# A decoder layer on one core: x, c and the bias vectors laid out by features before the launch, the first norm from squares and ones products, the opening in another order

## Chip, core and metric

The kernel runs on one core of a Trainium2 chip. The metric is the device time of one execution in microseconds (us), the median of several runs. Engines: TensorE (PE in the profile, its weight loads PEld), VectorE (DVE), ScalarE (ACT), GpSimd (POOL) and SyncE (SP), which only issues DMAs here.

## What is computed

One layer of a decoder for 1024 prompt tokens and 8 sample tokens, D = 1024 features, hidden width 2816, all in float32. What matters here is the first of its three norms and the first up-projection:

```python
mod = (silu(c) @ ada_w + ada_b).reshape(B, 9, D)      # c: one row for the prompt, one for each sample
def pre(i, t):                                         # i = 0, 1, 2
    return rms_norm(t, norm_g[i]) * (1 + mod[3*i+1]) + mod[3*i]
x = x + 0.5 * mod[2] * swiglu(pre(0, x), ffn1_up, ffn1_down)
y, states = token_mix(pre(1, x), ...)                  # attention and gated branch
x = x + mod[5] * y
x = x + 0.5 * mod[8] * swiglu(pre(2, x), ffn2_up, ffn2_down)
y_prompt, y_sample = rms_norm(x, final_g)
```

## The kernel before

**Layout and pieces.** Activations lie by features: partition = feature within a block of 128, eight blocks k. Tokens lie in two halves p of 516 columns, each two quarters q of 258 (256 prompt tokens and 2 samples); the sample columns are the `ends` of a quarter. `XT[p][h]` holds features 4h to 4h+3 of half p. Matmuls run in three parts: an operand is split into a high part and a low remainder (`high` on ScalarE, `low` on VectorE), and hi*hi, hi*lo, lo*hi are added up, so a block of four k is 12 matmuls of 128 x 258 (L743 to L745).

**First up-projection.** `Up.run` goes through 22 column blocks n. Blocks 0 and 1 go plainly, half by half, in turns (0, p=0), (1, p=0), (0, p=1), (1, p=1) of eight steps each; steps 0 to 3 need features 0 to 3 (h = 0) of the half, steps 4 to 7 features 4 to 7, and after each of the last four the PSUM result is read (L767, L768, L771). From block 2 on a turn has seven products over both halves (of 24 matmuls), whose operands `blend` makes from sums and differences of the blocks of x (eight passes of VectorE over 1032 columns for each half). `prepare` splits weights ahead of their use.

**What sets the order.** The program order on each engine is written out. Within a block, `tick` is called after each second k, so twice in a step; each tick advances the generators of `hi_q` by one `yield`. `require` advances them at once where a step needs what they make.

**The opening (L1012 to L1176).** SyncE loads ada weights of groups 0 and 2, four row tiles of x, the first up weights, ada groups 1 and 3, the second up weights, the other four row tiles. c, the ada bias and the norm weights come as rows and are transposed on TensorE (`silu_c`, L447). Each ada group gives four blocks of features of the modulation: `first_mods` (8 matmuls), a copy, four transposes, three steps on VectorE (`ada_fin`, L416). Groups 0 and 2 are shift and scale of features 0 to 3 of the first norm, groups 1 and 3 of features 4 to 7. For each row tile t, `row_scale` sums squares along the row on ScalarE and VectorE, `over_rms` scales the row, `turned_x` transposes it, `modulate` reads PSUM, scales and shifts. The samples go the same way (`sample_rows`, `sample_norm`). Steps 0 to 3 of the first turn are written in between, step 0 and 1 ahead of ada group 3. The second half of the tokens follows as `second_half` in `hi_q`; in it `raw_x` (L1028) also transposes all eight unscaled row tiles, copies them out of PSUM and stores them to `xs_d`, from where `Down` (L843) loads the residual; only then come `blend(0)` and `blend(1)`.

**The other norms.** `pair_norm` (L625) makes norms 2 and 3 from x by features: `rstd` (L499) sums squares over partitions by products with a column of ones, takes the power on GpSimd, and small products spread the result over partitions (L630); then for each block a VectorE pass (L642) and a ScalarE pass (L643), and after four blocks one copy of the sample columns (L645).

Of the kernel before, what the change touches and what calls it, by code (L numbers as in the profile page):

```python
# [15 lines left out]
D = 1024  # L16
# [18 lines left out]
def const_block():  # L35
    c = np.zeros((128, C_END), np.float32)
    i = np.arange(128)
    neg = np.float32(-1e30)
    c[:, C_ID:C_ID + 128] = np.eye(128)
    c[:, C_MP:C_MP + 128] = np.where(i[None, :] >= i[:, None], 0, neg)  # L40
    c[:, C_MO:C_MO + 128] = np.where(i[None, :] <= i[:, None], 0, neg)
    c[:, C_M0:C_M0 + 128] = c[:, C_MO:C_MO + 128]
    same = (i[None, :] // 64) == (i[:, None] // 64)
    c[:, C_M2:C_M2 + 128] = np.where(same & (i[None, :] <= i[:, None]), 0, neg)
    for j in range(2):
        for h in range(2):
            c[2 * j + h, C_SEL + j * 128 + h * 64:C_SEL + j * 128 + h * 64 + 64] = 1
    for hh in range(4):
        c[:, C_SX + hh] = (i % 32) == hh
        c[:, C_BM + hh] = (i // 32) == hh  # L50
    return c
# [14 lines left out]
def trunk(ctx: ExitStack, tc, a, o):  # L66
# [72 lines left out]
    START = dict(sc=(4, 6, 5, 5), pt=(7,), ms=(6,), tr=(6, 7), nx=(0, 1, 2, 3))  # L139
# [209 lines left out]
    ada0, xin, XT = {}, {}, {}  # L349
# [34 lines left out]
    XS = cpool.tile([P, 8, 8], FT, name="XS")  # L384
# [62 lines left out]
    def silu_c():  # L447
        q = ps_ms()
        nc.tensor.transpose(q[:, :104], rows[:104, :128], ident[:104, :104])
        nc.vector.tensor_copy(RT, q[:, :104])  # L450
        q = ps_pt()
        for k in range(8):
            nc.tensor.transpose(q[:, k * 16:k * 16 + 9], crow[:, k * 128:(k + 1) * 128], ident[:9, :9])
        nc.vector.memset(ph[:, 256:512], 0.0)
        qv = q[:, :128].rearrange("p (k t) -> p k t", k=8)[:, :, :9]
        th = tt()
        t3 = th[:, :72].rearrange("p (k t) -> p k t", k=8)
        nc.scalar.activation(t3, qv, AF.Tanh, scale=0.5)
        nc.vector.scalar_tensor_tensor(t3, t3, 1.0, qv, op0=ALU.add, op1=ALU.mult)
        nc.vector.tensor_scalar(scf[:, :, :9], t3, 0.5, None, op0=ALU.mult)  # L460

    def row_stat(row, w, ss, n):

        for h in range(2):
            e = tt()
            v = row[:, h * 512:(h + 1) * 512]
            if h:
                nc.vector.scalar_tensor_tensor(e[:w, :512], v, 1.0, v, op0=ALU.mult, op1=ALU.mult,
                                               accum_out=ss[:w, 4 + n:5 + n])
            else:  # L470
                nc.scalar.activation(e[:w, :512], v, AF.Square, accum_out=ss[:w, n:n + 1])

    def row_rstd(ss, w, i, n):
        r = R0[:w, i:i + n]
        nc.vector.tensor_tensor(r, ss[:w, :n], ss[:w, 4:4 + n], op=ALU.add)
        nc.vector.tensor_scalar(r, r, 1.0 / D, EPS, op0=ALU.mult, op1=ALU.add)
        nc.gpsimd.tensor_tensor(r, r, nhalf[:w, :n], op=ALU.pow)
# [147 lines left out]
    def pair_norm(i, p, b0, blocks, slow):  # L625

        x = XT[p]
        rs = yield from rstd(p, BLOCKS, 4 if blocks and p else 5, 2 if p else 3)
        for v, (b, w) in zip(rs, BLOCKS):
            mm_f(PSB[:, b0 + b // QW, b % QW:b % QW + w], v.to_broadcast([w, 128]), ident[:w, :w], start=True, stop=True)  # L630
        pb = PSB[:, b0:b0 + 2, :QW]
        sh, gp = 24 * i, 24 * i + 8
        ts = tt()[:, :32].rearrange("p (k q t) -> p k q t", k=8, q=2)
        for h in range(2):
            u = ts[:, 4 * h:4 * h + 4]
            mod = lambda n: MOD[:, n + 4 * h:n + 4 * h + 4, 1 + 4 * p:5 + 4 * p].rearrange("p k (q t) -> p k q t", q=2)
# [12 lines left out]

# [193 lines left out]
    class Down:  # L843
        FIRST = [sum(PARTS[:i]) for i in range(len(PARTS))]

        def __init__(self, wd, src, res, gate, samples):
            wd = wd[0].rearrange("(k p) c -> p k c", p=128)
            self.src, self.res, self.gate, self.samples = src, res, gate, samples
# [33 lines left out]
        def hook(self, n, j, turns):  # L882
# [15 lines left out]
            elif j == 3:  # L898
                for p in range(2):
                    XT[p] = [four(qb(name="x")) for h in range(2)]  # L900
                for h in range(2):
                    for p in range(2):
                        src, x = self.res[:, 4 * h:4 * h + 4, p * PW:(p + 1) * PW], XT[p][h]
                        if self.samples is None:
                            nc.gpsimd.dma_start(x, src)
                            continue
                        for q in range(2):
                            nc.gpsimd.dma_start(x[:, :, q * QW:q * QW + 256], src[:, :, q * QW:q * QW + 256])
                        nc.gpsimd.tensor_copy(ends(x), self.samples[:, 4 * h:4 * h + 4, 4 * p:4 * p + 4].rearrange(
                            "p k (q t) -> p k q t", q=2))  # L910
# [73 lines left out]
    up1, down1 = Up(a["ffn1_up"], g_d), Down(a["ffn1_down"], g_d, xs_d, 16, XS)  # L984
# [26 lines left out]
    up2, down2 = Up(a["ffn2_up"], g_d), Down(a["ffn2_down"], g_d, x2_d, 64, None)  # L1011
# [14 lines left out]
    SXT, XN = {}, {}  # L1026

    def raw_x(t):  # L1028

        row = xin[t // 2][:, t % 2, :1024]  # L1030
        c0 = PW * (t // 4) + BLOCKS[t % 4][0]
        for h in range(2):
            q = bank("tr")
            for k in range(4):
                nc.tensor.transpose(q[:, k * 128:(k + 1) * 128], row[:, (h * 4 + k) * 128:(h * 4 + k + 1) * 128], ident)
            e = tt()[:, :512]
            nc.scalar.activation(e, q, AF.Copy)
            nc.gpsimd.dma_start(xs_d[:, 4 * h:4 * h + 4, c0:c0 + 128], e.rearrange("p (k t) -> p k t", k=4))

    def row_scale(t):  # L1040

        ss = small()
        row_stat(xin[t // 2][:, t % 2, :1024], 128, ss, 0)
        row_rstd(ss, 128, t, 1)

    def over_rms(t, h):

        if h == 0 and t % 2 == 0:
            XN[t // 2] = rows2(qb(name="xn"))
        src, dst = (v[t // 2][:, t % 2, h * 512:(h + 1) * 512] for v in (xin, XN))  # L1050
        r = R0[:, t:t + 1]
        if t % 2 == h:
            nc.scalar.activation(dst, src, AF.Copy, scale=r)
        else:
            nc.vector.tensor_scalar(dst, src, r, None, op0=ALU.mult)

    def turned_x(t, h, qs, ks=range(4)):

        for k in ks:
            f = h * 4 + k  # L1060
            nc.tensor.transpose(qs[k][:, t % 4 * 128:(t % 4 + 1) * 128], XN[t // 2][:, t % 2, f * 128:(f + 1) * 128], ident)

    def sample_rows():
        q = ps_pt()
        for k in range(8):
            nc.tensor.transpose(q[:, k * 8:(k + 1) * 8], srow[:, k * 128:(k + 1) * 128], ident[:8, :8])
        nc.vector.tensor_copy(XS, q[:, :64].rearrange("p (k t) -> p k t", k=8))
        ss = small()
        row_stat(srow, 8, ss, 0)
        row_rstd(ss, 8, 8, 1)  # L1070
        e = tt()
        yield
        nc.vector.tensor_scalar(e[:8, 64:72], ident[:8, :8], R0[:8, 8:9], None, op0=ALU.mult)
        yield
        q = ps_ms()
        for k in range(8):
# [886 lines left out]
```

## Time and profile before

| | before |
|---|---|
| median of 3 runs | 2377.33 us (2374.25 to 2377.36) |
| the profiled execution | 2377.03 us, its span 2375.2 us |
| TensorE busy | 2337.8 us, 98% of the span |
| VectorE busy | 1291.1 us, 54% |
| ScalarE busy | 768.8 us, 32% |
| GpSimd busy | 250.6 us, 11% |

Times are counted from the start of the span. "Busy" of TensorE counts overlapping, pipelined matmuls once; a matmul of 128 x 258 is shown with some 0.28 us, while the next starts 0.12 us later. PEclk is the clock that TensorE was granted, 1.00 being 2.4 GHz and 0.50 being 1.2 GHz. In brackets behind an instruction stands how long its engine had been idle, and what ended that.

### The profile page before, as it was taken

The page shows a single profiled execution, that of the slowest core. Times are in us where ns is not written, and L with a number is a line of the kernel's source. Part 1 is how long each engine was busy: PE and PEld are TensorE (multiplying, and loading weights), DVE is VectorE, ACT ScalarE, POOL GpSimd, SP SyncE. Part 2 cuts the span into 40 slices and gives each one's busy share as a digit, 9 for nine tenths or more (in the row PEclk, how much of TensorE's full clock was granted, in tenths as well). Part 3 has the DMA queues.
Part 4 walks back from the last instruction along what each step waited for, and adds up shares of the span by engine and source line. Part 5 has one row for each costly group of instructions (what it writes and reads, how often), then busy time and mean ns, then how long its engine had stood idle before and what let it go on. Part 6 is the DMA issues. An engine that isn't in the chain of part 4 may idle for free.

```text
span 2375.2 us, 42343 instructions
## 1 busy us (share of the span) xinstructions
PE 2337.8 (98%) x17999; PEld 2253.4 (95%) x17999; DVE 1291.1 (54%) x2687; ACT 768.8 (32%) x1466; POOL 250.6 (11%) x374
## 2 busy tenths in 40 slices
PE   7899999999999999999999999999999999999999
PEld 5899999999999999999998999999999999999998
DVE  5655555665565544333252525635766666665665
ACT  4533333333111443444421122224433333331112
POOL 1200000001000200011110012221000000010003
PEclk8999999999999999999999999999999999999999
DMA  8555555447311311133221127534255555363101
GB/s 298 126 159 174 163 171 186 138 161 267 125 36 54 107 39 56 55 89 102 86 78 59 41 79 229 175 125 125 72 196 187 186 187 187 110 239 125 54 19 72
DMA packets 203606, 305.00 MB, mean 128 GB/s; under 512 B 9017, under 2 KB 145953, under 8 KB 199834
## 3 DMA queue, kind: packets, MB, share of 16 engines
q1 hardware_dynamic: 177840, 206.38, 26.4%
q0 software_dynamic: 25424, 95.83, 12.4%
q8 instruction: 141, 2.31, 0.4%
q14 instruction: 47, 0.39, 0.1%
q10 hardware_dynamic: 154, 0.09, 0.0%
HBM read 245.72 MB, written 100.53 MB: 146 GB/s over the span
## 4 chain that ended last, share of the span: by engine, by line
PE 62%; DVE 2%; ACT 1%; issue 0%; DVEq 0%; POOL 0%; ACTq 0%
PE PSB L287 7%; PE PSB L288 6%; PE PSB L289 6%; PE PSB L743 6%; PE PSB L744 6%; PE PSB L745 6%; PE PSB L303 3%; PE PSB L304 3%; PE PSB L305 3%; PE PSB L320 3%; PE PSB L321 3%; PE PSB L319 3%; PE PSB L1343 1%; PE PSB L1395 1%; PE PSB L1378 1%; PE PSB L1592 1%
## 5 line engine op out<-in xcount | busy, mean ns | idle before, releaser
L287 PE MATMUL PSB<-n,hi 128*128 128x258 f32 (+1 forms) x1152 | 361.5, 314 | 1.8 <-DVE s L933 1.8
L743 PE MATMUL PSB<-h,lo 128*128 128x258 f32 x1248 | 356.9, 286 | 4.6 <-DVE t L768 4.2
L743 PE MATMUL PSB<-h,hi 128*128 128x258 f32 x1248 | 355.9, 285 | 2.5 <-DVE t L771 2.5
L744 PE MATMUL PSB<-h,lo 128*128 128x258 f32 x1248 | 353.2, 283 | 0.3 <-DVE h L576 0.3
L744 PE MATMUL PSB<-h,hi 128*128 128x258 f32 x1248 | 352.9, 283 | 0.0
L745 PE MATMUL PSB<-h,lo 128*128 128x258 f32 x1248 | 352.3, 282 | 0.0
L745 PE MATMUL PSB<-h,hi 128*128 128x258 f32 x1248 | 352.1, 282 | 0.0
L288 PE MATMUL PSB<-n,hi 128*128 128x258 f32 (+1 forms) x1152 | 348.7, 303 | 0.6 <-DVE n L549 0.6
L289 PE MATMUL PSB<-n,lo 128*128 128x258 f32 (+1 forms) x1152 | 347.1, 301 | 0.0
L320 PE MATMUL PSB<-g,hi 128*128 128x344 f32 x864 | 276.6, 320 | 0.0
L321 PE MATMUL PSB<-g,lo 128*128 128x344 f32 x864 | 276.4, 320 | 0.0
L319 PE MATMUL PSB<-g,hi 128*128 128x344 f32 x864 | 275.8, 319 | 0.0
L743 PEld LDWEIGHTS PSB<-h,lo 128*128 128x128 f32 x1248 | 236.4, 189 | 18.4 <-issue 10.1
L743 PEld LDWEIGHTS PSB<-h,hi 128*128 128x128 f32 x1248 | 235.9, 189 | 14.8 <-issue 11.7
L287 PEld LDWEIGHTS PSB<-n,hi 128*128 128x128 f32 x1152 | 217.9, 189 | 22.5 <-issue 17.0
L744 PEld LDWEIGHTS PSB<-h,lo 128*128 128x128 f32 x1248 | 236.7, 190 | 0.5 <-DVE h L576 0.5
L744 PEld LDWEIGHTS PSB<-h,hi 128*128 128x128 f32 x1248 | 236.2, 189 | 0.0
L745 PEld LDWEIGHTS PSB<-h,lo 128*128 128x128 f32 x1248 | 236.1, 189 | 0.0
L745 PEld LDWEIGHTS PSB<-h,hi 128*128 128x128 f32 x1248 | 235.7, 189 | 0.0
L249 ACT ACTIVATE hi<-raw 128x1024 fp32r<-128x1024 f32 (+1 forms) x114 | 114.8, 1008 | 349.7 <-PE PSB L320 314.9
L288 PEld LDWEIGHTS PSB<-n,hi 128*128 128x128 f32 x1152 | 218.3, 189 | 1.9 <-DVE n L549 1.7
L289 PEld LDWEIGHTS PSB<-n,lo 128*128 128x128 f32 x1152 | 218.1, 189 | 0.0
(300 smaller groups left out, 4434.0 us busy)
## 6 DMA issues: line engine op xcount, KB each, us to landing
raw<-in_ffn_up_dram SPq DMA_DIRECT2D x88, 512.0 KB, 5.1
ada<-in_ada_w_dram SPq DMA_DIRECT2D x36, 1024.0 KB, 5.4
out_dram<-in_cache_kv_g_dram SPq DMA_DIRECT2D x16, 2047.0 KB, 11.1
g<-g_d POOLq DMA_DIRECT2D x22, 1032.0 KB, 6.8
g_d<-t POOLq DMA_DIRECT2D x80, 258.0 KB, 2.7
raw<-in_ffn_down_dram SPq DMA_DIRECT2D x16, 1024.0 KB, 5.0
raw<-in_w_in_dram SPq DMA_DIRECT2D x12, 1024.0 KB, 5.5
raw<-in_w_in_dram SPq DMA_DIRECT2D x18, 512.0 KB, 4.7
```

The lines of the kernel that those rows point to most:

```text
L249: nc.scalar.activation(h3, v, AF.Copy)
L287: mm_f(ps, wh, ah, start=(k == 0), stop=False)
L288: mm_f(ps, wh, al, start=False, stop=False)
L289: mm_f(ps, wl, ah, start=False, stop=(k == K - 1))
L303: mm_f(ps[:, q, :], wh, h, start=(k == 0), stop=False)
L304: mm_f(ps[:, q, :], wh, l, start=False, stop=False)
L319: mm_f(ps[:, c], wh, h[:, cs], start=(k == 0), stop=False)
L320: mm_f(ps[:, c], wh, l[:, cs], start=False, stop=False)
L321: mm_f(ps[:, c], wl, h[:, cs], start=False, stop=(k == K - 1))
L743: mm_f(out, wh, ah, start=(kk == 0 and start), stop=False, **go)
L744: mm_f(out, wh, al, start=False, stop=False, **go)
L745: mm_f(out, wl, ah, start=False, stop=(kk == 3 and stop), **go)
```

## The change

`kernel()` now lays x out on the host as it is used on the chip (`x_cols`, 128 x 8 x 1032) and packs ada bias, norm weights, final weights and c, by features, into one array (`f_cols`). On the chip all transposes of x, of c and of the bias rows are gone, and so are `raw_x`, the row sums, the scaled rows and the special path of the samples. The first norm is made from x by features: `squares` (ScalarE and VectorE square, VectorE sums: 5 VectorE passes and 2 ScalarE passes over 1032 columns for a half), then `rstd`, `spread` and `norm_half`, which are the former `pair_norm` cut in pieces. `norm_half` copies the sample columns after every second block and not after four; norms 2 and 3 use it too. `Down` loads its residual from `x_cols`. The order of the opening, its loads and its PSUM banks are new.

```diff
+def token_columns(x_prompt, x_sample):
+    c = np.empty((128, 8, NT), np.float32)
+    xp, xs = by_rows(x_prompt), by_rows(x_sample)
...
-    START = dict(sc=(4, 6, 5, 5), pt=(7,), ms=(6,), tr=(6, 7), nx=(0, 1, 2, 3))
+    START = dict(sc=(0, 1, 6, 6), pt=(7,), ms=(6,))
...
+    def load_x(p):
+        for h in range(2):
+            for k in range(0, 4, 2):
+                nc.sync.dma_start(XT[p][h][:, k:k + 2], a["x_cols"][:, 4 * h + k:4 * h + k + 2, p * PW:(p + 1) * PW])
...
+    nc.scalar.dma_start(ph[:, 512:688], a["f_cols"])
+    nc.scalar.dma_start(cst[:, :C_M0], a["consts"][:, :C_M0])
...
     def pair_norm(i, p, b0, blocks, slow):
-        x = XT[p]
         rs = yield from rstd(p, BLOCKS, 4 if blocks and p else 5, 2 if p else 3)
...
+        pb = spread(rs, b0)
         for h in range(2):
...
+            yield from norm_half(i, p, h, pb)
             if blocks:
                 yield from halves(p, h, 1 + slow)
         yield from blend(p) if blocks else split_rows(p, slow)
...
+    def norm_half(i, p, h, pb):
+        x = XT[p][h]
+        sh, gp = 24 * i, 24 * i + 8
+        u = tt()[:, :16].rearrange("p (k q t) -> p k q t", k=4, q=2)
...
+        for k in range(4 * h, 4 * h + 4):
+            v = x[:, k % 4]
+            nc.vector.scalar_tensor_tensor(two(v), two(v), MOD[:, gp + k, 0:1], pb, op0=ALU.mult, op1=ALU.mult)
+            nc.scalar.activation(v, v, AF.Identity, bias=MOD[:, sh + k, 0:1])
+            if k % 2:
+                nc.vector.tensor_copy(ends(x)[:, k % 4 - 1:k % 4 + 1], u[:, k % 4 - 1:k % 4 + 1])
+            yield
...
-                        src, x = self.res[:, 4 * h:4 * h + 4, p * PW:(p + 1) * PW], XT[p][h]
...
+                        nc.gpsimd.dma_start(XT[p][h], self.res[:, 4 * h:4 * h + 4, p * PW:(p + 1) * PW])
...
-    load_ada0(0, 1)
+    XT[0] = [four(qb(name="x")) for h in range(2)]
+    load_x(0)
+    load_ada0(0)
     load_ada0(2)
-    for t in range(4):
-        load_x(t)
     up1.load(0)
-    for grp in (1, 3):
-        load_ada0(grp)
+    load_ada0(1)
+    load_ada0(3)
     up1.load(1)
-    for t in range(4, 8):
-        load_x(t)
+    XT[1] = [four(qb(name="x")) for h in range(2)]
+    load_x(1)
...
+    def squares(p):
+        sq = qb(name="sq")
+        acc = ph[:, 688:688 + 2 * PW]
+        flat = lambda h, k: XT[p][h].rearrange("p k t -> p (k t)")[:, k * PW:(k + 2) * PW]
+        s0, s1 = sq[:, :2 * PW], sq[:, 2 * PW:4 * PW]
         for h in range(2):
+            nc.scalar.activation(s0, flat(h, 0), AF.Square)
+            nc.vector.scalar_tensor_tensor(s1, flat(h, 2), 1.0, flat(h, 2), op0=ALU.mult, op1=ALU.mult)
+            yield
+            if h == 0:
+                nc.vector.tensor_tensor(acc, s0, s1, op=ALU.add)
+            else:
+                nc.vector.tensor_tensor(acc, acc, s0, op=ALU.add)
+                nc.vector.tensor_tensor(acc, acc, s1, op=ALU.add)
+            yield
+        accp[p] = [acc[:, :PW], acc[:, PW:]]
...
+    steps(squares(0))
+    pb = spread(steps(rstd(0, BLOCKS, 0, 0)), 4)
+    for g in (0, 2):
+        steps(mods[g])
+        steps(fins[g], 1)
+    for g in (0, 2):
+        steps(fins[g])
+    rows_ = norm_half(0, 0, 0, pb)
+    first = halves(0, 0, 1, 2)
+    steps(rows_, 2)
+    steps(first, 1)
     up1.prepare(0)
...
+    steps(rows_)
+    steps(first, 1)
     up1.prepare(1)
     steps(first)
...
     up1.step(0, 0, 0)
     up1.prepare(2)
     up1.step(0, 1, 0)
...
+    steps(mods[1])
+    steps(fins[1], 1)
     up1.step(0, 2, 0)
     up1.prepare(3)
...
+    steps(fins[1])
     up1.step(0, 3, 0)
...
+    steps(mods[3])
+    steps(fins[3])
+    steps(norm_half(0, 0, 1, pb))
     steps(halves(0, 1, 1, 2))
...
     def second_half():
...
+        yield from rest(6)
+        yield from squares(1)
+        yield from pair_norm(0, 1, 6, True, 0)
         ada_q.append(ada_stream())
...
     dealing(**UPPER)
+    dealing(ms=(4,))
+    hi_q.append(blend(0))
     hi_q.append(second_half())
```

## Rows read from the trace of the kernel before

**Rows 1.** Stretches: length, then busy us (instructions) of PE, PEld, DVE, ACT, POOL; PEclk, DMA share, GB/s

```profile
44.67:110.50 65.83, 57.13 (x460) 54.34 (x459) 46.65 (x75) 38.62 (x64) 18.77 (x27) 1.00 0.49 110
64.00:87.00 23.00, 18.59 (x150) 17.19 (x150) 7.55 (x10) 12.62 (x22) 12.94 (x18) 1.00 0.79 158
87.00:110.50 23.50, 20.42 (x168) 20.00 (x167) 22.25 (x29) 11.70 (x18) 1.74 (x4) 1.00 0.27 53
110.50:160.00 49.50, 49.50 (x408) 45.59 (x407) 29.87 (x49) 16.83 (x30) 3.42 (x5) 1.00 0.62 196
...
1740.00:1800.00 60.00, 60.00 (x502) 60.00 (x502) 37.35 (x58) 21.94 (x39) 4.29 (x6) 1.00 0.53 185
```

**Rows 2.** Timeline, three landmarks: start us, length us, engine, line, operation

```profile
34.13 0.39 PE L743 MATMUL PSB<-h,lo 128*128 128x258 f32 x1
...
44.67 0.39 PE L743 MATMUL PSB<-h,lo 128*128 128x258 f32 x1
...
110.57 0.60 ACT L792 ACTIVATE t<-PSB 128x516 f32<-128x516 f32 x1 [1.03 <-PE PSB L745]
```

**Rows 3.** Waits of PE, 0 to 125 us: total us, times, longest

```profile
PE PSB L1035 <- ACT t L1037: 4.4, 6, 1.5
...
PE PSB L743 <- DVE t L768: 2.7, 1, 2.7
```

**Rows 4.** Groups by line, PE in 64 to 87 us: busy us, mean ns, idle before

```profile
L1035 PE MATMUL PSB<-cst,xin 128*128 128x128 f32 x64 | 9.2, 279 | 4.4 <-ACT t L1037 4.4
```

**Rows 5.** Timeline, the two last loads waited for: ada group 2, row tile 3

```profile
15.96 1.06 PE L397 MATMUL PSB<-ada,ph 128*32 128x512 f32 x8 [0.83 <-DMA ada<-in_ada_w_dram]
...
21.14 0.63 ACT L471 ACTIVATE t<-xin 128x512 f32<-128x512 f32 x1 [0.62 <-DMA xin<-in_x_prompt_dram]
```

**Rows 6.** Timeline, finishing an ada group, and two groups' products

```profile
22.58 1.06 PE L425 MATMUL PSB<-cst,t 128*128 128x128 f32 x4
...
23.67 0.31 DVE L429 TENSOR_REDUCE MOD<-PSB 128x36 f32<-128x144 f32 x1 [2.06 <-PE PSB L425]
...
24.25 0.20 DVE L434 SCALAR_TENSOR_TENSOR MOD<-MOD,ph 128x36 f32<-128x36 f32 x1
...
31.23 2.96 PE L397 MATMUL PSB<-ada,ph 128*32 128x512 f32 x16
...
39.67 0.60 ACT L419 ACTIVATE t<-PSB 128x512 f32<-128x512 f32 x1 [2.77 <-PE PSB L397]
```

**Rows 7.** Stretches, for the clock: the opening, and behind ones products

```profile
20.00:33.00 13.00, 10.34 (x48) 7.54 (x52) 6.68 (x22) 4.88 (x10) 2.28 (x3) 0.50 1.09 362
...
784.00:788.00 4.00, 4.00 (x31) 3.97 (x31) 0.21 (x2) 0.00 (x0) 1.72 (x2) 0.57 0.02 4
```

**Rows 8.** Chain that ended last: start us, us, the ones products of a norm

```profile
1647.95 2.94 PE PSB L507 x36
```

**Rows 9.** Timeline, a norm of 781 to 790 us: the two powers, spreading

```profile
784.65 1.72 POOL L511 TENSOR_TENSOR s<-s,mis 128x4 f32<-128x4 f32 x2 [9.41 <-DVE s L510]
...
788.09 1.58 PE L630 MATMUL PSB<-cst,s 128*128 128x128 f32 x12
```

**Rows 10.** Single lines and one tile: ns min/median/max, first and last start us

```profile
L537 DVE TENSOR_TENSOR h<-x,h x30: 1225/1227/1233, 34.7 to 1702.9; 128x1032 fp32r<-128x1032 f32 x30
L533 ACT ACTIVATE h<-x x30: 1043/1060/1076, 33.6 to 1701.3; 128x1032 fp32r<-128x1032 f32 x30
L642 DVE SCALAR_TENSOR_TENSOR x<-x,MOD,PSB x32: 739/747/751, 791.4 to 1668.4; 128x516 f32<-128x516 f32 x32
L643 ACT ACTIVATE x<-x,MOD x32: 712/728/733, 792.1 to 1669.1; 128x516 f32<-128x516 f32 x32
L576 DVE TENSOR_TENSOR h<-x,h x4: 689/692/697, 32.7 to 45.3; 128x516 fp32r<-128x516 f32 x4
```

**Rows 11.** Timeline, the copy of the sample columns in a later norm

```profile
1606.25 0.18 DVE L645 COPY x<-t 128x16 f32<-128x16 f32 x1 [0.80 <-ACT x L643]
```

**Rows 12.** Waits of PE behind 125 us: total us, times, longest

```profile
PE PSB L303 <- DVE s L933: 1.8, 1, 1.8
```

More of the change, by code (lines that the diff above doesn't have):

```diff
@@ L50, in const_block, with by_rows, small_columns @@
         c[:, C_BM + hh] = (i // 32) == hh
+    return c
+def by_rows(v):
+    return v.reshape(-1, 8, 128).transpose(2, 1, 0)
+def small_columns(c_prompt, c_sample, ada_b, norm_g, final_g):
+    cols = [v.reshape(-1, 128).T for v in (ada_b, norm_g, final_g)]
+    cols.append(by_rows(np.concatenate([c_prompt, c_sample]).reshape(9, 1024)).reshape(128, 72))
+    return np.ascontiguousarray(np.concatenate(cols, axis=1))
+def token_columns(x_prompt, x_sample):
+    c = np.empty((128, 8, NT), np.float32)
+    xp, xs = by_rows(x_prompt), by_rows(x_sample)
+    for i in range(4):
+        c[:, :, i * QW:i * QW + 256] = xp[:, :, i * 256:i * 256 + 256]
+        c[:, :, i * QW + 256:i * QW + QW] = xs[:, :, 2 * i:2 * i + 2]
     return c
@@ L447, in silu_c @@
     def silu_c():
[L448 to L453, printed above, removed]
         nc.vector.memset(ph[:, 256:512], 0.0)
-        qv = q[:, :128].rearrange("p (k t) -> p k t", k=8)[:, :, :9]
+        cv = ph[:, 616:688].rearrange("p (k t) -> p k t", k=8)
         th = tt()
         t3 = th[:, :72].rearrange("p (k t) -> p k t", k=8)
-        nc.scalar.activation(t3, qv, AF.Tanh, scale=0.5)
-        nc.vector.scalar_tensor_tensor(t3, t3, 1.0, qv, op0=ALU.add, op1=ALU.mult)
+        nc.scalar.activation(t3, cv, AF.Tanh, scale=0.5)
+        nc.vector.scalar_tensor_tensor(t3, t3, 1.0, cv, op0=ALU.add, op1=ALU.mult)
         nc.vector.tensor_scalar(scf[:, :, :9], t3, 0.5, None, op0=ALU.mult)
[L462 to L477, printed above, removed]
     BLOCKS = [(0, 128), (128, 128), (QW, 128), (QW + 128, 128), (256, 2), (QW + 256, 2)]
@@ L983, in trunk @@
     x2_d = dp.tile([P, 8, NT], FT, name="x2_d")
-    up1, down1 = Up(a["ffn1_up"], g_d), Down(a["ffn1_down"], g_d, xs_d, 16, XS)
+    up1, down1 = Up(a["ffn1_up"], g_d), Down(a["ffn1_down"], g_d, a["x_cols"], 16)
     win = a["w_in"][0].rearrange("(k p) c -> p k c", p=128)
@@ L1025, in trunk @@
+    load_x(1)
     nc.sync.dma_start(cst[:, C_M0:], a["consts"][:, C_M0:])
[L1026 to L1031, printed above, removed]
-        for h in range(2):
[L1033 to L1076, printed above, removed]
-            mm_f(q[:, k * 8:(k + 1) * 8], srow[:, k * 128:(k + 1) * 128], e[:8, 64:72], start=True, stop=True)
-        SXT[0] = v = e[:, :64].rearrange("p (k t) -> p k t", k=8)
-        nc.vector.tensor_copy(v, q[:, :64].rearrange("p (k t) -> p k t", k=8))
@@ L1097, in steps @@
     def steps(g, n=99):
         for _ in range(n):
-            if next(g, 0) == 0:
-                return
+            try:
+                next(g)
+            except StopIteration as e:
+                return e.value
     silu_c()
@@ L1959 @@
     arrays["consts"] = const_block()
+    x_cols = token_columns(arrays.pop("x_prompt"), arrays.pop("x_sample"))
+    arrays["x_cols"] = x_cols
+    arrays["f_cols"] = small_columns(*[arrays.pop(n) for n in ("c_prompt", "c_sample", "ada_b", "norm_g")],
+                                     arrays["final_g"])
     nc = build({n: v.shape for n, v in arrays.items()})
```

138 lines of the change are left out of this document (12 added, 126 removed).

## The prediction, made before the change was run

> **What bounds the kernel now.** I read the table of stretches first, then the opening in order of time, then the waits of TensorE. From 110.5 us on TensorE is busy without a gap [rows 1], and the change leaves its products there as they are, so a microsecond won or lost ahead of that point moves the end by a microsecond. The reader should mark three points [rows 2]: the first product of the first up-projection starts at 34.13; step 4 of its first turn (`Up.step`, the first to need features 4 to 7) starts at 44.67; the first joint product of column block 2 has ended when ScalarE reads it at 110.57. I call the last two S and E. Between them lie 28 steps of 12 matmuls and one product of 24, 360 matmuls. The undisturbed pace is 60.00 us for 502, 0.1195 us each [rows 1], so 43.0 us are needed and 65.8 are spent: 22.8 us are overhead. The waits and the line of `raw_x` say where most of it lies: 64 transposes of raw x, 9.2 us of busy time, and 4.4 us of TensorE waiting for the copies out of PSUM between them [rows 3, 4]. In 87.00 to 110.50 VectorE is busy 22.25 of 23.5 us [rows 1]: there `blend` holds TensorE up, with one wait of 2.7 us [rows 3].
>
> **What is removed, and the opening in its new order.** All transposes of x and c go, the row sums of squares, the scaled copies, the stores of transposed x to DRAM. In their place come, for each half p of the tokens, five passes over 1032 columns (`squares`), 24 tiny matmuls (`rstd`, 6 blocks by 2 parts, each two instructions), 12 of `spread`, then `norm_half`. For p = 0 all of `squares`, `rstd` and `spread` stand ahead of the ada products in TensorE's program, and groups 1 and 3 of ada now come after steps 1 and 3 of the first turn.
>
> The loads bind no earlier than before: when row tile 3 of x had landed, at 21.14, the queue had moved four ada pieces and four x pieces, 6 MB; by the same bytes the new order has x of p = 0 and ada groups 0 and 2. Between 15.96 and 21.14 the last four x pieces, 2 MB, came in [rows 5], so x of p = 0, first in the new order, lands at about 10.5 (the time at which as many bytes were in before, 15.96 less 5.2, is 10.8).
>
> Then, added up: VectorE's last three passes of `squares` at 1.23 [rows 10], the first on landing: 14.2. The ones products ran 36 in 2.94 at the full clock [rows 8], 0.082 each. TensorE has done nothing by then, and where its work was sparse before (20 to 33) it had clock 0.50 [rows 7]; at half speed 24 take 3.9 (up to 6.4, if each took what a transpose took there, 0.265 [rows 6]): 18.1. Scaling and first power 1.1, since two powers took 1.72 [rows 9]: 19.2. Spread, 12 in 1.58 at full clock [rows 9], 3.2 at half: 22.4. Ada groups 0 and 2, 16 in 2.96 [rows 6]: 25.4, with their data there since 21. Finishing both: two runs of four transposes at 1.06 through one bank, a reduction of 0.31 between, then reduction to last modulation step (23.67 to 24.45): 28.7 [rows 6]. `norm_half`: 0.5 for the sample columns, two passes of VectorE (0.75, the second 0.66 later), one of ScalarE 0.73, the copy of the ends 0.18, then the high part (about 0.6) and the low part 0.69 [rows 10, 11]: step 0 starts at about 33, a microsecond ahead of 34.13. But its second half needs features 2 and 3, whose passes stand on VectorE behind that copy and those low parts: some 4 us later, 37.
>
> From there TensorE runs, at 0.1195 a matmul, half of step 0 (0.7), step 1 (1.45), ada 1 (1.0), step 2 (1.45), four transposes (0.6), step 3 (1.45), ada 3 (1.0): 44.6. Behind ada 3 nothing is left to run, and this chain is bare: copy 0.6 [rows 6], transposes 0.6, 0.78 on VectorE, 0.5, two passes 1.4, ScalarE 0.73, copy 0.18, two passes 1.4, ScalarE 0.73, high and low parts 1.3, less the 0.7 by which step 4 may start on the high part: 7.6. S comes at 52.2, or at 55 if steps 0 and 1 still run at half clock. I take 53.5: **8.8 us late**. In the kernel before this chain was covered by steps 2 and 3 and by transposes.
>
> **From S to E.** Behind that gap of TensorE the first matmuls go at half clock. A dip behind the ones products lasted 3.4 us (4 us at a mean of 0.57 [rows 7]), which costs 1.7. *The Trainium skill, TensorE: Matmul & The Clock Gate, section "Why this matters for your kernels", says that a TensorE left idle between bursts falls back to the lower of its clock levels; by it a gap like the one ahead of S costs a dip. The trace agrees as far as it goes: the clock was 0.50 in 20 to 33, behind idle and sparse work. No run here shows the gap of S itself; without its dip the sum is 1.7 lower.*
> Counted from S (a tick is half a step, 0.72): turn 0 ends at 5.8 + 1.7 = 7.5. `second_half` rests six ticks, so `squares` of p = 1 stands on VectorE behind the read-out of step 6, whose product ends at 6.05 and is read by 6.9: two passes (2.46), a read-out (0.4), three more passes (3.5, the starts a little closer than the ends): 13.3, where the ones products wanted it at 12.3: 1.0 of wait. Ones 2.0; two ticks, 1.5; spread 1.6 to 3.2, I take 2.1: 18.9. `norm_half` of features 0 to 3: 0.5, 1.4, 0.73, 0.18, again 1.4, 0.73, 0.18, and a read-out of 0.4: 24.4; high part 1.06 and low part 1.23 of a quarter [rows 10]: 26.7. Turn 2 wants it eight ticks and one dip (1.7) after spread, at 26.4: 0.3. The other quarter's low part ends 1.2 later; features 4 to 7 take the same 5.1, two read-outs (0.8) and 2.3 more: 36.1, where turn 2 step 4 wants them four steps (5.8) after 26.7, at 32.5: 3.6. From there VectorE has what it did in 87 to 110.5, 22.25 us, and the three passes of `blend` that it had done earlier, 3.7, together 26 us, while TensorE has 168 matmuls, 20.1: 5.9 too much, of which banks not yet needed hide some; I take 4.5 (0 to 8). Overhead: 1.7 + 1.0 + 2.0 + 2.1 + 1.7 + 0.3 + 3.6 + 4.5 = 16.9. S to E: 43.0 + 16.9 = 59.9 in place of 65.8, **5.9 us won back**.
>
> **The later norms.** `norm_half` is also what the second and third norms now run, and it copies the ends after each pair of features, not after four. Each of 8 added copies stands on VectorE behind a ScalarE pass just issued, and what waits behind it is the next pair's passes and the read-out of the running products (L927, L1830). Today's copy waited 0.80 [rows 11]. So the bounds are 0 (all under TensorE's products) and 8 x 0.8 = 6.4; VectorE's lateness does reach TensorE in these stages (L303 waits 1.8 for L933 [rows 12]). I take **2.7**. No gain is possible: nothing is taken out there. The residual load of `Down` drops a step on GpSimd and reads longer runs; TensorE shows no wait on that load, so 0.
>
> **Sum.** 8.8 - 5.9 + 2.7 = +5.6 us, against the profiled execution's 2377.03 us (span 2375.2): 2382.6. The three runs' median, 2377.33, is 0.3 above it. A measurement of this kernel can tell about 0.2%, 4.8 us, from no change, so the forecast lies just beyond it.
>
> **The rivals.** (a) *The transposes come back in full.* If p = 1 is ready in time, S to E holds only what TensorE itself does anew: 43.0 + ones 2.0, spread 2.1, two dips 3.4 = 50.5, which wins 15.3; with S at 51.5 (full clock in the opening) 6.8 late and the later copies hidden: -8.5, 2368.5. It decides at one point: turn 2 step 4 starts without waiting for the low part of features 4 to 7. For it: ScalarE loses the 16 copies of `raw_x`, and VectorE was busy only 7.55 of 23 us in 64 to 87 [rows 1]. Against it: `squares` is issued only after six ticks. (b) *A wash.* S at 51.5, or a smaller backlog, later copies hidden: 6.8 - 5.9 = +0.9, 2378. (c) *Worse:* S at 55 (+10.3), a backlog of 8 (-2.4), copies all bare (+6.4): +14.3, 2391.3.
>
> **How the numbers follow.** Forecast, slower by 4.8 to 10 us (its own range 2382 to 2387), 0.38, (c) 0.12, (b) 0.33, (a) 0.17: faster 0.17, the same 0.33, slower 0.50. The range leaves out the far part of (a) and of (c): 2369 to 2391.
>
> **What would show it.** Right, if step 4 of turn 0 starts near 53.5 with TensorE idle ahead of it behind ada group 3; if no L1035 or L1061 is left and E lies about 3 us later than 110.5; if the copies of the ends wait twice as often in the later norms. Wrong, if step 4 starts before 49 (then ada 3's chain was not bare), if E comes ahead of 106 (rival a), or if TensorE waits on loads in the opening, which I cost at nothing.

## The result: 18 us slower, twelve more than forecast

The changed kernel takes 2395.4 us (median of 4 runs, 2394.13 to 2399.66) where the kernel before, run beside it, takes 2377.35: a ratio of 1.0079, interval 1.0068 to 1.0091. It is slower, as forecast, but by 18 us instead of 5.6, and outside the range that ended at 2391. The profiled execution took 2394.13 us, its span 2392.4: 17.2 longer than the span before.

Landmarks of the changed kernel, from its timeline (start us, length us, engine, line, operation, idle time before it with what ended it). Lines are those of the changed kernel: L740 to L742 are the matmuls of `block`, L564 the high part of a piece, L789 the read-out of a joint product, L324 to L327 and L309 to L311 the products of Down and of the input projection.

```profile
12.97 3.84 PE L496 MATMUL PSB<-mis,ph 128*128 128x1 f32 x24 [12.97 <-DVE ph L1031]
...
21.11 4.95 PE L409 MATMUL PSB<-ada,ph 128*32 128x512 f32 x32
...
32.59 0.58 PE L740 MATMUL PSB<-h,lo 128*128 128x258 f32 x1 [4.83 <-ACT lo L710]
...
46.32 1.92 PE L409 MATMUL PSB<-ada,ph 128*32 128x512 f32 x16
48.96 0.66 PE L437 MATMUL PSB<-cst,t 128*128 128x128 f32 x4 [0.72 <-ACT t L431]
55.86 0.58 PE L740 MATMUL PSB<-h,lo 128*128 128x258 f32 x1 [6.24 <-ACT h L564]
...
123.15 0.60 ACT L789 ACTIVATE t<-PSB 128x516 f32<-128x516 f32 x1 [0.59 <-PE PSB L742]
```

Against [rows 2], the first step starts earlier (32.59 for 34.13), S comes 11.2 us later (55.86 for 44.67) and E 12.6 later (123.15 for 110.57). So all of the loss but 4.6 us (17.2 - 12.6) has happened when the joint products begin. No transpose of x is left in the opening.

The stretches (length, busy us with instructions of PE, PEld, DVE, ACT, POOL, then the granted clock, DMA share, GB/s): first S to E, then 123.15 to 160, then four short stretches inside S to E.

```profile
55.86:123.15 67.29, 58.86 (x398) 56.74 (x399) 51.45 (x77) 29.19 (x42) 5.76 (x9) 0.83 0.10 30
123.15:160.00 36.85, 36.85 (x304) 33.92 (x303) 22.20 (x36) 13.48 (x25) 2.00 (x3) 1.00 0.69 219
...
56.00:61.00 5.00, 4.85 (x21) 4.55 (x22) 4.82 (x8) 3.75 (x7) 0.00 (x0) 0.50 0.01 2
71.50:78.50 7.00, 7.00 (x40) 6.73 (x40) 0.22 (x2) 0.00 (x0) 1.70 (x2) 0.51 0.00 0
95.50:102.50 7.00, 6.36 (x30) 6.36 (x31) 6.93 (x8) 3.70 (x6) 0.00 (x0) 0.51 0.00 0
119.50:123.00 3.50, 3.49 (x17) 3.19 (x17) 3.50 (x6) 1.37 (x2) 0.54 (x1) 0.53 0.11 38
```

Read the clock, not the busy share. S to E took 67.3 us with 62 fewer instructions on TensorE than before (398 for 460 in [rows 1]). The granted clock was 0.83, where all of it ran at 1.00 before. The four short stretches stand at 0.50 to 0.53, the lower of the two levels (1.2 GHz): about 22 us of S to E, which cost some 11, and TensorE counts as busy in nearly all of them. A reader of the busy share alone sees 58.9 us of work there; 43.0 us of it are matmuls at the full clock. It is no accident of one execution: two kernels below that have the same opening (the copy after four rows, and the copies on GpSimd) took 67.6 and 66.7 us from S to E, with S at 56.8 and 57.8.

The waits of TensorE in 0 to 140 us (what it waited for: us in total, times, longest), to be read against [rows 3]:

```profile
PE PSB L740 <- ACT h L564: 8.0, 2, 6.2
PE PSB L740 <- ACT lo L710: 4.8, 1, 4.8
PE PSB L740 <- ACT h L522: 3.8, 2, 2.2
PE PSB L740 <- DVE t L765: 1.9, 1, 1.9
PE PSB L741 <- DVE h L526: 1.8, 2, 0.9
```

And behind 140 us, to be read against [rows 12], where the first of these lines was 1.8:

```profile
PE PSB L325 <- DVE s L923: 4.1, 2, 2.8
PE PSB L325 <- DVE s L1729: 3.7, 1, 3.7
PE PSB L740 <- DVE t L768: 2.5, 2, 2.1
PE PSB L740 <- DVE t L765: 2.4, 1, 2.4
```

### The profile page after: what moved, and what is told of

The parts are those of the page before. It is cut to its first block, busy times and chain, and to the rows that moved or that the text cites. A ratio compares the mean times of both kernels' runs of the same rounds, so it can differ in the third digit from the quotient of the medians.

```text
span 2392.4 us, 42019 instructions
## 1 busy us (share of the span) xinstructions
PE 2334.2 (98%) x17910; PEld 2251.6 (94%) x17910; DVE 1298.8 (54%) x2683; ACT 758.9 (32%) x1436; POOL 231.6 (10%) x345
## 4 chain that ended last, share of the span: by engine, by line
PE 91%; DVE 5%; ACT 2%; issue 1%; DMA 1%; POOL 0%; SPq 0%; DVEq 0%; ACTq 0%
PE PSB L740 12%; PE PSB L741 12%; PE PSB L742 12%; PE PSB L309 7%; PE PSB L310 6%; PE PSB L311 6%; PE PSB L342 6%; PE PSB L343 6%; PE PSB L341 6%; PE PSB L325 4%; PE PSB L327 4%; PE PSB L326 4%; PE PSB L409 2%; ACT x L642 1%; DVE h L526 1%
## 5 line engine op out<-in xcount | busy, mean ns | idle before, releaser
L740 PE MATMUL PSB<-h,lo 128*128 128x258 f32 x1248 | 359.2, 288 | 21.0 <-ACT h L564 8.0
L309 PE MATMUL PSB<-n,hi 128*128 128x258 f32 (+1 forms) x1152 | 361.8, 314 | 2.0 <-DVE s L923 1.7
L740 PE MATMUL PSB<-h,hi 128*128 128x258 f32 x1248 | 357.4, 286 | 2.5 <-DVE t L768 2.5
L742 PE MATMUL PSB<-h,lo 128*128 128x258 f32 x1248 | 354.6, 284 | 0.0
L742 PE MATMUL PSB<-h,hi 128*128 128x258 f32 x1248 | 353.1, 283 | 0.0
L311 PE MATMUL PSB<-n,lo 128*128 128x258 f32 (+1 forms) x1152 | 347.4, 302 | 0.0
L740 PEld LDWEIGHTS PSB<-h,lo 128*128 128x128 f32 x1248 | 238.7, 191 | 35.8 <-issue 10.9
L740 PEld LDWEIGHTS PSB<-h,hi 128*128 128x128 f32 x1248 | 237.8, 191 | 14.7 <-issue 11.5
L741 PEld LDWEIGHTS PSB<-h,lo 128*128 128x128 f32 x1248 | 239.2, 192 | 3.0 <-DVE h L526 2.2
L309 PEld LDWEIGHTS PSB<-n,hi 128*128 128x128 f32 x1152 | 217.8, 189 | 23.0 <-issue 16.9
L742 PEld LDWEIGHTS PSB<-h,lo 128*128 128x128 f32 x1248 | 238.8, 191 | 0.3 <-DVE lo L711 0.3
L742 PEld LDWEIGHTS PSB<-h,hi 128*128 128x128 f32 x1248 | 237.4, 190 | 0.0
L311 PEld LDWEIGHTS PSB<-n,lo 128*128 128x128 f32 x1152 | 217.7, 189 | 0.0
```

The costliest lines, as they stand in the source:

```text
L309: mm_f(ps, wh, ah, start=(k == 0), stop=False)
L311: mm_f(ps, wl, ah, start=False, stop=(k == K - 1))
L740: mm_f(out, wh, ah, start=(kk == 0 and start), stop=False, **go)
L741: mm_f(out, wh, al, start=False, stop=False, **go)
L742: mm_f(out, wl, ah, start=False, stop=(kk == 3 and stop), **go)
```

## The experiments

Three questions: what the removed transposes were worth by themselves, what the clock cost, and what the added copies cost. Each time below is a median of 5 runs or more, beside runs of the kernel before on the same chip (medians of those 2374.7 to 2377.3), so ratios are compared; landmarks are those of one profiled execution.

**The removal alone: the kernel before, with x by features for the residual only.**

```diff
-up1, down1 = Up(a["ffn1_up"], g_d), Down(a["ffn1_down"], g_d, xs_d, 16, XS)
+up1, down1 = Up(a["ffn1_up"], g_d), Down(a["ffn1_down"], g_d, a["x_cols"], 16, None)
 def second_half():
...
-        for t in range(8):
-            raw_x(t)
-            yield
```

> The kernel before with its own opening, and one part of the change alone: the first Down product's residual comes from x laid out by features, so the 64 transposes of raw x, their 16 copies and 16 stores, and GpSimd's copies of the sample columns are gone. The opening is as before, step 4 at 44.7 us. Theory: the 64 transposes (9.2 us on TensorE) and most of the 4.4 us of waits in them come back, less 2 to 4 us where the second pair's VectorE work is now late instead: the first joint product's read-out at 99 to 103 instead of 110.6 us, 2366 to 2370 us. Rival: VectorE's second half sets the read-out as well: read-out at 107 or later, 2374 us or more.

Measured: 2360.34 us, ratio 0.9935 (0.9923 to 0.9948), faster than either kernel, and by more than was expected. Its read-out of the first joint product and its stretch from the same S:

```profile
96.99 0.60 ACT L805 ACTIVATE t<-PSB 128x516 f32<-128x516 f32 x1 [3.21 <-PE PSB L758]
```

```profile
44.67:97.00 52.33, 49.78 (x400) 48.02 (x400) 48.00 (x78) 30.09 (x50) 7.30 (x12) 1.00 0.25 75
```

E is 13.6 us earlier than in [rows 2], as much as the 9.2 us of transposes and the 4.4 us of waits of [rows 3, 4] add up to. The stretches divide it otherwise: against [rows 1] TensorE's busy time falls by 7.4 us (57.13 to 49.78) and its idle time by 6.2 (8.7 to 2.6), since pipelined transposes overlap with the matmuls beside them and the joint product waits less as well. VectorE's work on the second pair, which I had let eat 2 to 4 us of it, was ready nearly in time in the old order. So this half of the change is worth 14 us, and the rest of it costs some 32.

**The order of the opening.** Ada group 1 ahead of step 0, group 3 behind it, the norm of features 4 to 7 ahead of steps 2 and 3.

```diff
 up1.prepare(0)
+steps(mods[1])
...
+steps(fins[1], 1)
 up1.step(0, 0, 0)
+steps(mods[3])
+steps(fins[3], 1)
+steps(fins[1])
 up1.prepare(2)
 up1.step(0, 1, 0)
-steps(mods[1])
-steps(fins[1], 1)
+steps(fins[3])
+steps(norm_half(0, 0, 1, pb))
+up1.prepare(3)
 up1.step(0, 2, 0)
-up1.prepare(3)
-steps(fins[1])
 up1.step(0, 3, 0)
-steps(mods[3])
-steps(fins[3])
-steps(norm_half(0, 0, 1, pb))
 steps(halves(0, 1, 1, 2))
```

> The changed kernel with its opening in another order: ada group 1 ahead of step 0 (TensorE idles 27.8 to 32.6 us there), group 3 behind step 0, and the norm of features 4 to 7 ahead of steps 2 and 3, so that TensorE's steps cover VectorE's and ScalarE's chain again. Theory: the 11.2 us by which step 4 comes later than before are the uncovered chain behind ada group 3; step 4 then starts at 50 to 51 instead of 55.9 us, the gap ahead of it shrinks to 2 us or less, the read-out of the first joint product comes 5 to 8 us earlier (115 to 118), 2387 to 2390 us. Rival: VectorE and ScalarE themselves set step 4 (they have the same passes to run): step 4 at 55 or later, 2395 us.

Measured: 2388.91 us, ratio 1.0058 (1.0046 to 1.0071).

```profile
52.40 0.39 PE L740 MATMUL PSB<-h,lo 128*128 128x258 f32 x1 [3.89 <-ACT h L564]
...
116.01 0.60 ACT L789 ACTIVATE t<-PSB 128x516 f32<-128x516 f32 x1 [0.36 <-PE PSB L742]
```

S at 52.4, not 50 to 51, and 3.9 us of the gap are left: part of the chain was uncovered by the order, part is VectorE's and ScalarE's own. E comes 7.1 us earlier, twice what S gained: the half clock around S is shorter (0.50 from about 53.5 to 57 us instead of 51 to 61), and from S to E it is 10 us in all instead of 22. Part of that is lost again, as one product ahead of the read-out waits 4.5 us for VectorE instead of 1.9.

**The clock by itself.** The changed kernel with 44 products that nobody reads in the gap ahead of step 4.

```diff
+for n in range(44):
+    kk = n % 4
+    mm_f(PSB[:, 6, :QW], up1.wt[0][0][:, kk * 128:(kk + 1) * 128], OPS[0][0][:, kk * QW:(kk + 1) * QW],
+         start=True, stop=True)
 steps(norm_half(0, 0, 1, pb))
```

> The changed kernel with 44 idle products (128x128 weights, 258 columns, into a bank that nobody reads) on TensorE in its gap of 6.2 us ahead of step 4. Theory (the clock): the half clock from 51.1 to 61.3 us is a result of the gap; with the gap filled step 4 still starts at 55.9 us, but its 48 products run at 0.117 instead of 0.21 us, so the steps behind it end 2.5 to 3 us earlier, and the first joint product's read-out comes at about 120.5 instead of 123.2: 2392.5 us. Rival: the half clock comes whatever TensorE does there, or VectorE's work on the second pair sets the end anyway: 2395 us, read-out at 123.

Measured: 2393.24 us, ratio 1.0071 (1.0057 to 1.0085). Its landmarks and stretches:

```profile
58.30 0.38 PE L740 MATMUL PSB<-h,lo 128*128 128x258 f32 x1 [1.03 <-ACT h L564]
...
120.52 0.60 ACT L789 ACTIVATE t<-PSB 128x516 f32<-128x516 f32 x1 [0.34 <-PE PSB L742]
```

```profile
58.30:120.50 62.20, 52.31 (x398) 50.59 (x399) 51.07 (x76) 28.95 (x42) 5.77 (x9) 0.95 0.11 33
51.00:58.00 7.00, 5.87 (x48) 5.66 (x48) 4.11 (x12) 3.40 (x6) 0.00 (x0) 1.00 0.19 46
58.00:63.00 5.00, 4.36 (x34) 4.16 (x35) 4.54 (x7) 4.08 (x8) 0.00 (x0) 1.00 0.02 5
71.50:78.50 7.00, 7.00 (x65) 6.82 (x64) 2.06 (x7) 0.88 (x2) 1.71 (x2) 1.00 0.01 2
```

The read-out comes at 120.52, where the clock's theory had it; by the rival it would have stayed at 123. The same 398 instructions take 62.2 us instead of 67.3. The stretch of half clock behind the gap is gone. The two that followed it did not come either; one of 3.4 us came at 85 instead, so that 6.8 us of S to E are at half clock and not 22. This is more than the theory spoke of, and part of it is lost again: one product ahead of the read-out waits 4.5 us for VectorE instead of 1.9. S itself came 2.4 us later in this execution: step 0 already starts 1.7 later (34.28), ahead of anything that was edited, and the half clock in steps 0 and 1 lasted until 44 instead of 41. The time as a whole moved by 2 us only, less than these runs can tell apart; the profiled execution, the slowest of its five (2397.11), has 34 us of half clock behind E, that of the changed kernel 17. So it is shown that the gap brings the half clock behind it; what the gap costs in the total is not.

How much a gap costs where nothing else is going on was measured in the kernel before, in the unbroken run of the first up-projection:

```diff
 down1.hook(n, j, len(up1.turns))
+if n in (12, 16, 20, 24) and j == 4:
+    e = tt()
+    nc.scalar.activation(two(e), up1.tmp["d"], AF.Copy)
+    for _ in range(3):
+        nc.scalar.activation(e, e, AF.Copy)
+    mm_f(PSB[:, 7, :8], e[:, :128], e[:, :8], start=True, stop=True)
```

> The kernel before with four gaps put into TensorE's unbroken run between 125 and 780 us: in four turns of the first up-projection one small product waits for a chain of four ScalarE copies behind product 4's copy, some 3 to 3.5 us; nothing else is changed (the small product's result is not read). It measures the price of a gap by itself. Theory: each gap also brings a stretch of half clock of some 3 us or more behind it, so it costs 1.5 to 2 us more than it lasts: four gaps of 3.3 us cost 19 to 22 us, 2394 to 2398 us. Rival: a gap costs what it lasts, 13 us, 2389 us, and the clock stays at 1.00.

Measured: 2393.7 us, ratio 1.0071 (1.0057 to 1.0085). The trace has three of the four gaps: the up-projection ends ahead of the turn that was to hold the last. For three, the expectations are 14 to 16.5 us more (theory) and 10 (rival).

```profile
311.03 0.39 PE L1205 MATMUL PSB<-t 128*128 128x8 f32 x2 [3.35 <-ACT t L1204]
...
406.70 0.39 PE L1205 MATMUL PSB<-t 128*128 128x8 f32 x2 [3.40 <-ACT t L1204]
...
500.08 0.60 PE L1205 MATMUL PSB<-t 128*128 128x8 f32 x2 [3.41 <-ACT t L1204]
```

```profile
311.00:315.00 4.00, 3.97 (x21) 3.97 (x22) 0.69 (x1) 1.02 (x2) 0.00 (x0) 0.59 0.01 4
315.00:319.00 4.00, 4.00 (x35) 4.00 (x35) 2.17 (x4) 0.00 (x0) 0.71 (x1) 0.98 0.02 7
...
407.00:411.00 4.00, 4.00 (x21) 2.48 (x20) 0.69 (x1) 0.17 (x1) 0.00 (x0) 0.57 0.01 4
...
499.00:506.00 7.00, 5.92 (x27) 5.92 (x28) 0.69 (x1) 2.03 (x4) 0.00 (x0) 0.53 0.00 0
```

E and the first product of the input projection, in this kernel, and that product in the kernel before:

```profile
112.33 0.61 ACT L792 ACTIVATE t<-PSB 128x516 f32<-128x516 f32 x1 [1.05 <-PE PSB L745]
...
830.31 0.36 PE L287 MATMUL PSB<-n,hi 128*128 128x258 f32 x1 [1.80 <-DVE s L933]
```

```profile
811.16 0.36 PE L287 MATMUL PSB<-n,hi 128*128 128x258 f32 x1 [1.79 <-DVE s L933]
```

Each gap brought a stretch at 0.50: about 3.4, 3.4 and 6.8 us long. From E to the first product of the input projection this kernel takes 717.98 us (112.33 to 830.31), the kernel before 700.59 (110.57 to 811.16): 17.4 more for 10.2 us of gaps. The 13.6 us at half clock cost 6.8, and 10.2 and 6.8 make 17.0 of the 17.4. A gap of 3.4 us costs 5.8, as the mean of three. The Trainium skill, TensorE: Matmul & The Clock Gate, section "Why this matters for your kernels", says that TensorE falls back to the lower clock when it idles between bursts; the three gaps agree. What lies behind the gap, 2.4 of the 5.8 us, is what the prediction counted too seldom. Not every wait brings it: behind one of 2.7 us in the kernel before [rows 3] the clock stayed at 1.00.

**VectorE's late work on the second pair.** The squares of the second pair in the opening, and no rests in front.

```diff
+steps(squares(1))
 steps(mods[3])
...
 def second_half():
-    yield from rest(6)
-    yield from squares(1)
     yield from pair_norm(0, 1, 6, True, 0)
```

> The changed kernel with the five passes of squares for the second half of the tokens moved into the opening, ahead of ada group 3, where VectorE and ScalarE idle, and without the six rests in front of them. Theory (VectorE's late work on the second pair): step 4 comes at 56 to 57 us, 0.5 to 1 later; the waits of 1.6, 0.9, 2.2, 0.9 and 2.0 us ahead of the first joint product mostly go, and with them the half clock of 95.5 to 102.3; from step 4 to the read-out 59 to 61 instead of 67.3 us, read-out at 115 to 118, 2388 to 2390 us. Rival (the clock alone): the waits go, but half clock behind the ones and the gap keeps the read-out at 121 or later, 2393 us or more.

Measured: 2387.43 us, ratio 1.0055 (1.0043 to 1.0067); S at 58.45, the gap ahead of it 7.50.

```profile
58.45:115.55 57.10, 51.45 (x398) 50.34 (x399) 46.76 (x73) 27.07 (x40) 6.32 (x10) 0.94 0.16 51
86.00:90.00 4.00, 3.74 (x18) 3.74 (x19) 4.00 (x6) 1.34 (x2) 0.54 (x1) 0.57 0.01 2
```

S to E falls from 67.3 to 57.1 us. Five waits of 7.5 us in all are replaced by one of 4.5 (for a read-out that stands on VectorE behind the norm's passes) and two below 1, and the stretches of half clock inside fall to the end of the one at S and the one shown, behind that wait. S pays 2.6 us, more than expected.

**The copies of the end columns.** Four kernels turn on the place of this copy. The first:

```diff
-            if k % 2:
+            if k % 2 and i == 0:
                 nc.vector.tensor_copy(ends(x)[:, k % 4 - 1:k % 4 + 1], u[:, k % 4 - 1:k % 4 + 1])
             yield
+        if i:
+            nc.vector.tensor_copy(ends(x), u)
```

> The changed kernel, but the later norms copy the two end columns once after four rows again, as the kernel before does; the opening's norms keep the copy after each pair. Theory: the extra copies, each of which makes VectorE wait about 0.8 us for ScalarE's activation, cost what is lost behind the opening, 17.2 - 12.6 = 4.6 us; so about 2395.4 - 4.6 = 2390.8 us, with TensorE's read of the first joint product still 123 us after the start. Rival: they are hidden and the 4.6 us has another source (the joint norms wait for the Down product's read-outs in either order): 2395 us, within 1 us.

Measured: 2387.93 us, ratio 1.0048 (1.0036 to 1.0061), so about 7 us less than the changed kernel. E comes at 124.35, no earlier than in the changed kernel; behind it the profiled execution is 8.7 us shorter. The four waits behind 140 us, in the order shown above:

```profile
PE PSB L325 <- DVE s L925: 2.0, 1, 2.0
PE PSB L325 <- DVE s L1731: 1.8, 1, 1.8
...
PE PSB L742 <- DVE t L770: 1.6, 2, 1.3
PE PSB L742 <- DVE t L767: 1.5, 1, 1.5
```

They fall from 12.7 to 6.9 us. The other way round, in the kernel before with the copy after each pair:

```diff
                 nc.scalar.activation(v, v, AF.Identity, bias=MOD[:, sh + k, 0:1])
+                if k % 2:
+                    nc.vector.tensor_copy(ends(x[h])[:, k % 4 - 1:k % 4 + 1], ts[:, k - 1:k + 1])
                 yield
-            nc.vector.tensor_copy(ends(x[h]), ts[:, 4 * h:4 * h + 4])
```

> The kernel before with one part of the change alone: its later norms copy the end columns after each pair of rows. Theory: 4.6 us more than before, about 2382.0 us. Rival (hidden): 2377.4 us.

Measured: 2389.3 us, ratio 1.0057 (1.0044 to 1.0069): 13.6 us more than before by the ratio, three times the expectation; 9.5 of the 11.4 us that its profiled span is longer lie behind E. Its waits are those of the changed kernel (4.1, 3.7, 2.5, 2.4). VectorE ahead of one of them:

```profile
802.91 0.17 DVE L645 COPY x<-t 128x8 f32<-128x8 f32 x1 [0.85 <-ACT x L643]
802.99 1.41 DVE L642 SCALAR_TENSOR_TENSOR x<-x,MOD,PSB 128x516 f32<-128x516 f32 x2
805.25 0.17 DVE L645 COPY x<-t 128x8 f32<-128x8 f32 x1 [0.85 <-ACT x L643]
805.33 0.74 DVE L928 SCALAR_TENSOR_TENSOR x<-PSB,MOD,x 128x512 f32<-128x512 f32 x1
805.99 0.15 DVE L934 TENSOR_TENSOR s<-PSB,MOD 128x4 f32<-128x4 f32 x1
```

Each copy of 0.17 us keeps VectorE waiting 0.85 us for ScalarE's pass, and the read-out of the running Down product (L928, L934) stands behind two of them. TensorE's next Down product waits 2.65 us there. The added waits sum to about 7 us; the rest is the clock, which behind E falls to 0.50 eight times (around 789, 809, 819, 829, 847, 1604, 1632 and 1662), 27 us in all, where the kernel before has six such stretches, 20 us.

The third leaves the copies after each pair and changes their engine alone:

```diff
-                nc.vector.tensor_copy(ends(x)[:, k % 4 - 1:k % 4 + 1], u[:, k % 4 - 1:k % 4 + 1])
+                (nc.gpsimd if i else nc.vector).tensor_copy(ends(x)[:, k % 4 - 1:k % 4 + 1], u[:, k % 4 - 1:k % 4 + 1])
```

> The changed kernel, still with a copy of the end columns after each pair of rows in the later norms, but on GpSimd instead of VectorE. Theory: it is not the copy of 0.17 us that costs but VectorE standing in front of it until ScalarE has ended its pass; on GpSimd the waits ahead of the Down products' read-outs fall back (4.1 and 3.7 us to 2 or less each), and the time falls by 5 to 8 us as with the copy after four rows: 2387.5 to 2390.5 us. Rival: the order of the copies is not it, or GpSimd's copies hold up the next passes over the same rows: 2395 us.

Measured: 2388.07 us, ratio 1.0044 (1.0032 to 1.0057), and the waits on L923 and L1729 fall to 1.9 each:

```profile
PE PSB L325 <- DVE s L923: 1.9, 1, 1.9
PE PSB L325 <- DVE s L1729: 1.9, 1, 1.9
```

As many copies as in the changed kernel, on GpSimd's queue, cost nothing that shows (2388.07 for the 2387.93 of the copy after four rows): it is the place in VectorE's queue that costs. So three pairs of kernels differ in these copies alone, and behind E they differ by 8.7 us (the copy after four rows), 9.5 (the kernel before with pairs) and 7.2 (GpSimd). The 4.6 us between the kernel before and the changed kernel are too low a price: waits of TensorE behind E grow from some 9 to 16 us between them, but the execution of the changed kernel happened to have 17 us of half clock there and that of the kernel before 20.

The fourth puts the copy after four rows on GpSimd, in the kernel without the transposes:

```diff
-            nc.vector.tensor_copy(ends(x[h]), ts[:, 4 * h:4 * h + 4])
+            nc.gpsimd.tensor_copy(ends(x[h]), ts[:, 4 * h:4 * h + 4])
```

> The kernel before with the residual from x laid out by features (no transposes of raw x), and besides the later norms' copy of the end columns on GpSimd. Theory (VectorE's wait of 0.8 us at each of the remaining 8 copies reaches TensorE): 2 to 4 us below the 2360.3 us of the kernel without transposes. Rival: with one copy after four rows the wait is hidden: 2360 us within 1.5.

Measured: 2361.03 us, ratio 0.9933 (0.9921 to 0.9946). With one copy after four rows there was nothing left to win; the rival held.

**All three together.** The opening's other order and the copy after four rows are as shown above; the second squares move less far than above:

```diff
 steps(halves(0, 1, 1, 2))
+steps(squares(1))
...
 def second_half():
-    yield from rest(6)
-    yield from squares(1)
```

> The changed kernel with the opening's other order, the second squares directly behind the opening's norm without rests, and the later norms' copies after four rows. Theory: the three add up: step 4 at 50 to 51, read-out of the first joint product at 108 to 111 us, and 4.6 to 7 us less behind it: 2374 to 2378 us, about the time of the kernel before, so the layout's opening costs what the transposes saved. Rival: they overlap (what step 4 wins is lost again in the second pair's waits): 2382 us or more.

Measured: 2376.72 us, ratio 1.0009 (1.0000 to 1.0017); S at 51.09, E at 113.34.

```profile
51.09 0.38 PE L742 MATMUL PSB<-h,lo 128*128 128x258 f32 x1 [3.88 <-ACT h L564]
...
113.34 0.60 ACT L791 ACTIVATE t<-PSB 128x516 f32<-128x516 f32 x1 [3.19 <-PE PSB L744]
```

The time is where the theory had it, in part by luck, as E is 2 to 5 us later than expected: S to E is 62.3, with a wait of 3.0 for the second squares and the one of 4.5 for a read-out, so S's gain is partly lost again in the second pair, as the rival said; the part behind E is 7.5 us shorter than in the changed kernel, more than the 4.6 to 7 expected. What the removal of the transposes wins, this opening still loses.

## Why the prediction was right in sign and wrong in size

The direction and its place held: S late behind an uncovered ada group 3, part of it won back up to E, something lost in the later norms. By steps:

- **Up to step 0: right in its times, in one place by luck.** Predicted: ones products from 14.2 for 3.9 us, spread to 22.4, ada to 25.4, step 0 at 33, its second half at 37. Measured: 12.97 for 3.84, spread to 21.2, step 0 at 32.59, second half at 36.36. Ada groups 0 and 2 took 4.95 us for 32 instructions, where I had 2.96 for 16 (the 8 matmuls of a group are 16 instructions in the trace); spreading ended 1.2 us early and the steps between ada and step 0 took less than I had put for them, which made up for it. TensorE waits for no load there.
- **S: 11.2 us late for 8.8, over by 2.4.** The bare chain of 7.6 us behind ada group 3 measured 55.86 - 48.24 = 7.62. The term that failed is TensorE's run in front of it, 37 to 44.6 or 47.4, of which I took the middle. It ran from 36.36 to 48.24: at half clock until about 41, which was my upper case and costs some 2.3, and with 1.9 us for an ada group of 16 where I wrote 1.0, twice.
- **S to E: 67.3 us for 59.9, over by 7.4. The mis-sized term is the clock.** The waits were near in sum, 1.0 + 0.3 + 3.6 + 4.5 = 9.4 predicted, 0.8 + 2.5 + 3.1 + 1.9 = 8.3 measured, but that is luck: the second was 2.2 too low and the last 2.6 too high. Predicted were two dips costing 1.7 each, 3.4. Measured were four stretches of half clock, 5.4 us from S on and 6.8, 6.8 and 3.4 us, 22 in all; at half speed they cost 11, which is 7.6 more. I had taken the length of a dip from one row behind ones products [rows 7], and had put none behind the waits, though I counted on those waits. The filled gap shows where the first of the four comes from, the three gaps what a wait of some 3 us brings with it. At the full clock not all of the 11 us would come back, since VectorE holds TensorE up the more: the filled gap won 5.1 from S to E with 15 us less of half clock.
- **Later norms: 4.6 us for 2.7 between these two executions, but 7.2 to 9.5 by the copies alone, outside the bounds of 0 to 6.4.** The upper bound, 8 x 0.8, priced VectorE's lost time; a wait that reaches TensorE costs its own length and then the clock. The copies' place in the queue was the right cause. The premise that TensorE is busy without a gap from 110.5 us on does not hold behind 780 us: the kernel before itself waits some 9 us there, the wait of [rows 12] being one of several, and has six stretches of half clock, of which [rows 7] shows one.
- **Sum:** 2.4 + 7.4 + 1.9 = 11.7 us over, which is 17.2 - 5.6 within rounding.
- **Rivals.** That the transposes come back in full (a) holds for the removal, with the opening left as it was: E 13.6 us earlier. In the changed kernel it fell at the point named for it: step 4 of turn 2 waits 2.16 us. The worse case (c) had S at 55 and a larger backlog of VectorE; S came at 55.9, but the loss behind it was mostly the clock's, which no rival had.

What stays open: where exactly a stretch of half clock begins and how long it lasts differed between executions with much the same waits. Behind the ones products it stood from 71.6 to 78.4 in the changed kernel and not at all with the gap filled, and waits of some 2 us had one behind them in some places and none in others. So the second and third of the four stretches, and the clock's share behind 780 us, are not assigned to single waits.

## What to carry to other kernels

Price a wait on the engine that bounds the kernel by what it starts, not only by its length: here a gap of 3.4 us on TensorE cost 5.8 on average. Take a change apart before judging it: the new layout was worth 14 us and the new opening and the moved copies lost 32. On an engine that runs in order, look at what stands behind a small instruction that waits; eight more copies of 0.17 us cost 7 to 9.5 us, and nothing that shows once they stood in another queue.

## What the runs showed of the hardware

- A single gap of 3.35 to 3.41 us in TensorE's otherwise unbroken run brought 3.4 to 6.8 us at a granted clock of 0.50, so the three cost 5.8 us each on average instead of 3.4.
- 44 products that nobody reads, run in the gap, kept the clock at 1.00 from 51 to 63 us; S to E was 5.1 us shorter.
- Waits of 4.5 us for a read-out came with 3.4 to 6.8 us at 0.50 in four kernels (the gap filled, the opening's other order, the squares early, all three); behind one of 2.7 us in the kernel before the clock stayed at 1.00.
- The ones products (one column each) need not bring the clock down: with the gap filled they ran at 1.00, in 71.0 to 73.2, and it stayed there behind them.
